# Squares of the first norm added in pairs by VectorE, and uneven halves with TensorE sums in the last norm

## The chip, the cores and the metric

The kernel runs on one core of one Trainium2 chip. A core has five engines that each work through their own list of instructions in order and wait for one another through semaphores: TensorE (PE in the profile, its weight loads PEld), VectorE (DVE), ScalarE (ACT), GpSimd (POOL) and SyncE (SP), which here only issues DMAs. The metric is the device time of one execution in microseconds (us). Before the change the median of three runs was 1303.08 us (1302.94 to 1303.72).

## The reference

One inference step of a one-layer decoder: a prompt of 512 tokens and 8 sequences of 4 new tokens, D_MODEL = 1024. What matters here are its first and its last lines:

```python
def _rms_norm(x, g):
    xf = x.astype(jnp.float32)
    y = xf * lax.rsqrt(jnp.mean(xf * xf, axis=-1, keepdims=True) + RMS_EPS)
    return (y * g).astype(x.dtype)

h = _rms_norm(x, pre_mix_g)          # first norm: everything else needs h
m, new_buf, new_shift, new_wkv = _mixer(h, ...)   # conformer branch, RWKV-7 branch, merge
x = x + _rms_norm(m, post_mix_g)
h2 = _rms_norm(x, pre_ffn_g)
f = jnp.square(jax.nn.relu(h2 @ w_ff_up)) @ w_ff_down
x = x + _rms_norm(f, post_ffn_g)     # last norm: the output y
```

The mean runs over the 1024 channels of a token. All arithmetic is float32.

## The kernel before, in words

Channels lie on partitions, in KT = 8 blocks of 128; tokens lie along the columns. There are N2 = 544 token columns (512 + 32), and N1 = 552 with the 8 rows of shift state. Every product with weights splits both sides into a high and a low part and adds three matmuls (part_steps, L145 to L155; the matmul is L152, its output tile `lin`), so an output block needs 3 matmuls per block of the contracted side. Columns go in two halves: S1 = 276 + 276 in the first norm, S2 = 272 + 272 later.

A sum over channels goes over partitions as well as over blocks. The kernel adds over partitions with a float32 matmul whose weights are a matrix of 1/1024 (`avg`), which leaves the mean in every partition. `rsqrt` (L106 to L112) is then five operations: logarithm and exponential on ScalarE (recorded on L235), a square on ScalarE (L110), and two corrections on VectorE (L111, L112).

The first norm (L254 to L274): eight DMAs bring x, two blocks of half the columns each, with one weight block loaded behind each half. For each half ScalarE squares the eight blocks (L260, tile `sq`, four buffers), and TensorE adds each square into `ss` with a matmul of its own (L261), eight a half. After rsqrt, VectorE scales the blocks to `hf` (L269) and splits them into high and low parts (`xh` by ScalarE, L173; `xl` by VectorE, L174). The first weight products need these, and both halves of them stand in one list on each engine.

The last stage is w_ff_down (L1041 to L1061). Output blocks 0 to 5 are finished with both halves. For each, `down(j)` adds the product to the partial result `part[j]` (tile `f`, VectorE L1028), then acc_sq squares it on ScalarE (L880) and adds the square to `facc` on VectorE (L881). Blocks 6 and 7 (`last`) are held back so that half 0 of both comes first, 96 matmuls of 272 columns, and then half 1 of both. After each half, `rstd` makes one float32 matmul of `avg` with `facc` (L169, tile `aux`) and rsqrt. Then, for each of the eight blocks, VectorE scales it (L1059), adds the residual `m` (L1060), and SP writes it out (L1061). Half 0's closing operations run while TensorE works on half 1's products; half 1's have nothing to run beside.

The order on each engine is set by a scheduler when the program is built; at run time every engine keeps to it. The pool of `lin` tiles in this stage has three PSUM buffers and that of `aux` has two.

Of the kernel before, what the change touches and what calls it, by code (L numbers as in the profile page):

```python
# [8 lines left out]
F32 = mybir.dt.float32  # L9
F32R = mybir.dt.float32r  # L10
AF = mybir.ActivationFunctionType
ALU = mybir.AluOpType
MULT, ADD, SUB = ALU.mult, ALU.add, ALU.subtract

D = 1024
KT = 8
# [21 lines left out]

S1 = ((0, 276), (276, 276))
S2 = ((0, 272), (272, 272))  # L40

VECS = [("pre_mix_g", 8), ("post_mix_g", 8), ("pre_ffn_g", 8), ("post_ffn_g", 8), ("conv_b", 8),
        ("conv_ln_g", 8), ("conv_ln_b", 8), ("decay_base", 8), ("iclr_base", 8), ("k_k", 8),
# [19 lines left out]
def hybrid_step(ctx: ExitStack, tc: tile.TileContext, xT, hist, s0, win, wco, wro, wo, wup, wdn, lora,  # L63
                vecs, convw, cst, yo, convo, shifto, wkvp, wkvs):
    nc = tc.nc
    PSUM = bass.MemoryType.PSUM
    act = nc.scalar.activation
    tt, stt, ts = nc.vector.tensor_tensor, nc.vector.scalar_tensor_tensor, nc.vector.tensor_scalar
# [24 lines left out]
    rms_eps, ln_eps, gn_eps, kk_neg, kk_eps, kk_log = (epst[:, i:i + 1] for i in range(6))  # L93
# [12 lines left out]
    def rsqrt(rs, x, eps, t):  # L106

        tact(LNEXP, rs, x, AF.Ln, bias=eps)
        tact(LNEXP, rs, rs, AF.Exp, scale=-0.5)
        act(t, rs, AF.Square, scale=math.sqrt(0.5))  # L110
        stt(out=t, in0=x, scalar=eps, in1=t, op0=ADD, op1=MULT)  # L111
        stt(out=rs, in0=t, scalar=1.5, in1=rs, op0=SUB, op1=MULT)  # L112

    def con(name):
        o = COFF[name]
        return cs[:, o:o + dict(CONSTS)[name]]
# [3 lines left out]
    def wraw(src):  # L120
        raw = wp.tile([128, KT * 128], F32, name="raw", tag="raw", bufs=WR)
        nc.sync.dma_start(raw, src.rearrange("p k c -> p (k c)"))
        return raw

    def wload(src, paged=None):
        return wsplit(wraw(src), paged)

    def wsplit(raw, paged=None, upper=nc.scalar.copy):

        if paged is None:  # L130
            parts = [(wp.tile([128, KT * 128], F32R, name="whi", tag="whi"),
                      wp.tile([128, KT * 128], F32R, name="wlo", tag="wlo", bufs=WL))]
        else:
            parts = [tuple(paged.tile([128, N2], F32R, name=n, tag="pg") for n in ("wh", "wl")) for _ in range(2)]
        n = KT // len(parts)
        out = []
        for i, (hi, lo) in enumerate(parts):
            r = raw[:, i * n * 128:(i + 1) * n * 128]
            hi, lo = hi[:, 0:n * 128], lo[:, 0:n * 128]
            upper(hi, r)  # L140
            tt(out=lo, in0=r, in1=hi.bitcast(F32), op=SUB)  # L141
            out += [(hi[:, 128 * k:128 * k + 128], lo[:, 128 * k:128 * k + 128]) for k in range(n)]
        return out
# [13 lines left out]
    def part_mm(*args):  # L157
        for _ in part_steps(*args):
            pass
# [72 lines left out]
    def tact(name, *args, **kw):  # L232

        with tables(name):
            lastact[0] = act(*args, **kw)  # L235
        return lastact[0]
# [5 lines left out]
    with tc.tile_pool(name="p0", bufs=1) as p0, tc.tile_pool(name="q0", bufs=1, space=PSUM) as q0:  # L242
        start = tables(LNEXP)
        x = p0.tile([128, KT, N1], F32, name="x")
        for o, m in S1:
            for k in range(0, KT, 2):
                nc.sync.dma_start(x[:, k:k + 2, o:o + m], xT[:, k:k + 2, o:o + m])
            raws.append(wraw(win[order[len(ready)]]))
            ready.append(wsplit(raws[-1]))
        avg = p0.tile([128, 128], F32, name="avg")  # L250
        nc.vector.memset(avg, 1.0 / D)
        rs, rt = (p0.tile([128, N1], F32, name=n) for n in ("rs", "rt"))
        hfs = [p0.tile([128, N1], F32, name=f"hf{k}") for k in range(KT)]
        with start:  # L254
            for s, (o, m) in enumerate(S1):
                q = slice(o, o + m)
                ps = q0.tile([128, 512], F32, name=f"ss{s}")
                for k in range(KT):
                    sq = p0.tile([128, 276], F32, name="sq", bufs=4)
                    act(sq, x[:, k, q], AF.Square)  # L260
                    nc.tensor.matmul(ps[:, 0:m], avg, sq, start=k == 0, stop=k == KT - 1)  # L261
                rsqrt(rs[:, q], ps[:, 0:m], rms_eps, rt[:, q])
            nc.sync.dma_start(cs, cst)
            nc.sync.dma_start(cw, convw)
            for s, (o, m) in enumerate(S1):
                q = slice(o, o + m)
                for k in range(KT):
                    hf = hfs[k]
                    stt(out=hf[:, q], in0=x[:, k, q], scalar=nvec("pre_mix_g", k), in1=rs[:, q], op0=MULT, op1=MULT)  # L269
                    if s:  # L270
                        nc.scalar.copy(hf[:, N2:N1], x[:, k, N2:N1])
                    split_hl(h[k][0][:, q], h[k][1][:, q], hf[:, q])
                    if s:
                        nc.sync.dma_start(shifto[:, k, :], hf[:, T - 1:N2])  # L274
# [51 lines left out]
    def gate(j):  # L326

        i = 50 + j if j < KT else 34 + j
        g = cv.tile([128, N2], F32, name="g", tag="g")
        yield from win_steps(i, S2, lambda s, ps, o, m: nc.scalar.copy(g[:, o:o + m], ps))  # L330
        nc.scalar.dma_start(g_dr[j], g[:, 0:N2])


    with ExitStack() as c1:
# [7 lines left out]
        aux, ytx = dict(pool=qc, tag="aux"), dict(pool=qc, tag="yt")  # L342
# [15 lines left out]
        for i in range(2):  # L358
            q = slice(64 * i, 64 * i + 64)
            nc.scalar.copy(maskD[q, :, i, :], mask[q].rearrange("p (a t) -> p a t", a=2))  # L360
            nc.scalar.copy(maskP[64 * i:64 * i + 32, i, :], maskS[64 * i:64 * i + 32])
            for g in range(2):
                r, o = slice(64 * i + 32 * g, 64 * i + 32 * g + 32), 32 * g
# [53 lines left out]
        def glu_gate(j):  # L417
            sg = page("gsg", cv)
            yield from win_steps(8 + j, S2, lambda s, ps, o, m: nc.scalar.copy(sg[:, o:o + m], ps))
            glu["fresh"], glu["sg"] = (j, sg), sg  # L420

        def glu_val(j, sg):
# [7 lines left out]
            def evac(s, ps, o, m):  # L430
                n = min(m, T - o)
                tt(out=u[:, CW - 1 + o:CW - 1 + o + n], in0=ps[:, 0:n], in1=sg[:, o:o + n], op=MULT)
                if s:
                    tt(out=useg.rearrange("p (b f) -> p b f", f=SEG)[:, :, CW - 1:SEG],
                       in0=ps[:, n:m].rearrange("p (b t) -> p b t", t=TS), in1=sv(sg), op=MULT)
            yield from win_steps(j, S2, evac)
            nc.sync.dma_start(convo[j], u[:, T:EXT])
# [6 lines left out]
        def sum_steps(lhsT, x, evac, pool, tag):  # L444
            for s, (o, m) in enumerate(S2):
                ps = pool.tile([128, 512], F32, name=tag, tag=tag)[:, 0:m]
# [12 lines left out]
        def rates(p):  # L459
# [8 lines left out]
            for i, (d, b) in enumerate(((sg, "decay_base"), (a, "iclr_base"))):  # L468
                for s, (o, m) in enumerate(S2):
                    yield from part_steps([(up[0][:, i], up[1][:, i])], [ld], s, o, m,  # L470
# [293 lines left out]
        def groupnorm(p):  # L764
# [22 lines left out]
            yield  # L787
            for s, (oo, m) in enumerate(S2):
                yield from part_steps([(lhi, llo)], [lg], s, oo, m,
# [69 lines left out]
    ql = c2.enter_context(tc.tile_pool(name="ql", bufs=2, space=PSUM))  # L859
    pl2 = c2.enter_context(tc.tile_pool(name="pl2", bufs=3, space=PSUM))  # L860
# [5 lines left out]
    def temp(name):  # L866
        lc[0] += 1
        pool, tag = ((cv, "t0"), (cv, "t1"), (fp, "t2"))[lc[0] % 3]
        return pool.tile([128, N2], F32, name=name, tag=tag, bufs=1)
    aux = dict(pool=ql, tag="aux")  # L870

    ALL = slice(0, N2)
    HALF = tuple(slice(o, o + m) for o, m in S2)
# [9 lines left out]
    def rstd(rs, acc, eps, s):  # L883
        t = temp("rt")
        f32sum(con("avg"), acc, S2[s:s + 1],
               lambda _, ps, o, m: rsqrt(rs[:, o:o + m], ps, eps, t[:, o:o + m]), **aux)
# [18 lines left out]
    for j in range(KT):  # L905
        o = page("o")
# [14 lines left out]
    with tc.high_priority(offset=HP):  # L921
        acc, mean = keep("acc", "acc"), keep("mean", "rs2")
# [4 lines left out]
        acc = keep("acc", "xacc")  # L927
# [3 lines left out]
        rs = keep("rs", "rs")  # L931
# [36 lines left out]
    acc, xacc, rs, rs2 = (keep(n, n) for n in ("acc", "xacc", "rs", "rs2"))  # L968
# [52 lines left out]
    part = []  # L1021

    def down(j):
        f = part[j]

        def evac(s, ps, o, m):
            q = slice(o, o + m)
            tt(out=f[:, q], in0=ps, in1=f[:, q], op=ADD)  # L1028
            acc_sq(acc, j, f, q)
        return evac  # L1030

    for half in range(2):
        fhl = [None] * 16
# [5 lines left out]
        if half:  # L1039
            acc, rs = keep("facc", "acc"), keep("frs", "rs")  # L1040
        for j in range(KT if half == 0 else KT - 2):  # L1041
            w = wload(wdn[j, 2 * half]) + wload(wdn[j, 2 * half + 1])
            if half == 0:
                f = cv.tile([128, N2], F32, name="f", tag=("gsg", "g")[j]) if j < 2 else \
# [3 lines left out]
            else:  # L1048
                linear(w, fhl, S2, down(j))

    last = [(j, wload(wdn[j, 2], pg) + wload(wdn[j, 3], pg)) for j in (KT - 2, KT - 1)]
    for s in range(2):
        q = HALF[s]
        for j, w in last:
            part_mm(w, fhl, s, *S2[s], down(j), pl2, "lin")
        rstd(rs, acc, rms_eps, s)
        for j in range(KT):
            f = part[j][:, q]
            stt(out=f, in0=f, scalar=nvec("post_ffn_g", j), in1=rs[:, q], op0=MULT, op1=MULT)  # L1059
            tt(out=f, in0=f, in1=x1[j][:, q], op=ADD)  # L1060
            nc.sync.dma_start(yo[:, j, q], f)  # L1061
# [80 lines left out]
```

## Time and profile before

| | us |
|---|---|
| median of 3 runs | 1303.08 (1302.94 to 1303.72) |
| profiled execution, its own time | 1299.37 |
| its span, first to last instruction | 1297.6 |
| TensorE busy | 1238.4 (95%) |
| VectorE busy | 819.9 (63%) |
| ScalarE busy | 652.0 (50%) |
| GpSimd busy | 198.0 (15%) |
| mean granted clock of TensorE | 0.989 |

A timeline row gives start, duration, engine, line, operation, output<-input, shapes and a count; in brackets stands how long the engine sat idle before it and what ended that. Matmuls overlap: a row's duration includes filling and draining, and the distance between starts is what one costs. A float32 matmul with `avg` is recorded as two matmuls (x2). In a table of stretches the columns are the stretch, its length, busy time (number) of each engine, then the granted clock of TensorE (PEclk), the share of DMA and GB/s.

### The profile page before, as it was taken

What the parts mean: (1) busy time and instruction counts of PE and PEld (TensorE: products, weight loads), DVE (VectorE), ACT (ScalarE), POOL (GpSimd) and SP (SyncE); (2) the same over time, 40 slices, a digit from 0 to 9 for tenths busy, and PEclk for the clock granted to TensorE, in tenths of its full rate; (3) what the DMA queues carried; (4) which work ended last, traced back from release to release, by engine and by line L of the source; (5) the groups of instructions that cost most, each with busy time, mean ns of one, the idle gap of its engine ahead of it and who ended that gap; (6) DMA issues with size and microseconds to landing.
All of it is one profiled execution on the core that took longest, in us unless ns stands there. A gap on an engine that the chain in (4) does not pass through costs nothing. (4 is left out here: it accounts for less than half of the span.)

```text
span 1297.6 us, 23134 instructions
## 1 busy us (share of the span) xinstructions
PE 1238.4 (95%) x9154; PEld 1162.8 (90%) x9154; DVE 819.9 (63%) x1545; ACT 652.0 (50%) x1563; POOL 198.0 (15%) x286
## 2 busy tenths in 40 slices
PE   7989999999999999999999999999999999999995
PEld 6978888887978888787889999999999999999995
DVE  6889889855888898887677465658432122333345
ACT  7453747575563747538244382356554223554231
POOL 2224232221323233132201100000000000000000
PEclk9989999999999999999999999999999999999998
DMA  6313121120202121131115642361122332232332
GB/s 202 104 33 109 33 82 34 49 69 19 84 33 96 34 81 33 33 95 42 67 48 195 220 167 92 110 209 50 34 82 82 98 86 94 82 97 75 90 98 70
DMA packets 45181, 110.60 MB, mean 85 GB/s; under 512 B 7056, under 2 KB 16528, under 8 KB 45072
## 3 DMA queue, kind: packets, MB, share of 16 engines
q1 hardware_dynamic: 41344, 104.33, 25.6%
q10 hardware_dynamic: 3728, 4.79, 1.1%
q8 instruction: 72, 1.18, 0.4%
q14 instruction: 37, 0.30, 0.1%
HBM read 94.79 MB, written 14.32 MB: 84 GB/s over the span
## 5 line engine op out<-in xcount | busy, mean ns | idle before, releaser
L152 PE MATMUL lin<-xh,whi 128*128 128x272 f32 (+1 forms) x2096 | 616.2, 294 | 4.1 <-DVE r L394 2.0
L152 PE MATMUL lin<-xh,wlo 128*128 128x272 f32 (+1 forms) x2096 | 615.6, 294 | 0.6 <-DVE wlo L141 0.6
L152 PE MATMUL lin<-xl,whi 128*128 128x272 f32 (+1 forms) x2096 | 614.2, 293 | 0.4 <-DVE xl L174 0.2
L152 PEld LDWEIGHTS lin<-xh,whi 128*128 128x128 f32 x2096 | 397.0, 190 | 7.2 <-issue 2.9
L152 PEld LDWEIGHTS lin<-xl,whi 128*128 128x128 f32 x2096 | 396.5, 189 | 3.7 <-issue 1.4
L152 PEld LDWEIGHTS lin<-xh,wlo 128*128 128x128 f32 x2096 | 396.6, 189 | 3.1 <-issue 1.4
L141 DVE TENSOR_TENSOR wlo<-raw,whi 128x1024 fp32r<-128x1024 f32 x131 | 160.7, 1227 | 197.8 <-ACT whi L140 175.7
L292 DVE SCALAR_TENSOR_TENSOR c<-u,cw,c 128x512 f32<-128x512 f32 x240 | 188.0, 783 | 5.7 <-DVE c L292 1.2
L140 ACT CAST whi<-raw 128x1024 fp32r<-128x1024 f32 x76 | 79.7, 1049 | 122.7 <-PE lin L152 119.2
L140 POOL CAST whi<-raw 128x1024 fp32r<-128x1024 f32 x55 | 65.4, 1189 | 319.0 <-PE lin L152 182.9
L152 PE MATMUL lin<-xh,wl 128*128 128x272 f32 x240 | 69.4, 289 | 0.0
L152 PE MATMUL lin<-xl,wh 128*128 128x272 f32 x240 | 69.3, 289 | 0.0
L152 PE MATMUL lin<-xh,wh 128*128 128x272 f32 x240 | 69.2, 288 | 0.0
L1001 DVE TENSOR_TENSOR xl<-ff,xh 128x272 fp32r<-128x272 f32 x64 | 28.3, 442 | 55.9 <-ACT ff L1000 55.9
L687 ACT ACTIVATE SV<-ch,pc 64x64 f32<-64x64 f32 x128 | 39.6, 309 | 19.2 <-PE ch L683 17.8
L228 ACT ACT_TABLE_LOAD x37 | 47.5, 1283 | 1.8 <-PEq L1124 1.2
L152 PEld LDWEIGHTS lin<-xh,wl 128*128 128x128 f32 x240 | 45.2, 188 | 0.1
L152 PEld LDWEIGHTS lin<-xh,wh 128*128 128x128 f32 x240 | 45.2, 188 | 0.1
L152 PEld LDWEIGHTS lin<-xl,wh 128*128 128x128 f32 x240 | 45.1, 188 | 0.1
L681 ACT ACTIVATE SV<-ch 64x64 f32<-64x64 f32 x128 | 27.9, 218 | 33.6 <-PE ch L679 31.6
L760 POOL TENSOR_SCALAR st<-st,epS 128x64 f32<-128x64 f32 x64 | 39.9, 673 | 7.9 <-DVE rt L597 7.9
L998 ACT ACTIVATE ff<-lin 128x272 f32<-128x272 f32 x64 | 25.3, 395 | 29.6 <-PE lin L152 29.5
(274 smaller groups left out, 1830.4 us busy)
## 6 DMA issues: line engine op xcount, KB each, us to landing
raw<-win SPq DMA_DIRECT2D x58, 512.0 KB, 3.7
raw<-wup SPq DMA_DIRECT2D x32, 512.0 KB, 3.6
raw<-wdn SPq DMA_DIRECT2D x32, 512.0 KB, 3.6
g_dr<-g ACTq DMA_DIRECT2D x16, 272.0 KB, 2.9
raw<-wro SPq DMA_DIRECT2D x8, 512.0 KB, 3.7
raw<-wco SPq DMA_DIRECT2D x8, 512.0 KB, 3.6
raw<-wo SPq DMA_DIRECT2D x8, 512.0 KB, 3.6
x<-xT SPq DMA_DIRECT2D x8, 276.0 KB, 4.7
```

The costliest lines, as they stand in the source:

```text
L140: upper(hi, r)
L141: tt(out=lo, in0=r, in1=hi.bitcast(F32), op=SUB)
L152: nc.tensor.matmul(ps, a, b[:, o:o + m], start=k == 0 and i == 0, stop=k == n - 1 and i == 2)
L228: lastact[0] = nc.scalar.preload_act_table_set(name)
L292: stt(out=c[:, 0:T], in0=u[:, t:t + T], scalar=w[:, t:t + 1], in1=c[:, 0:T], op0=MULT, op1=ADD)
L681: nc.scalar.mul(SV[H[i], c, i, :], ch[H[i], 2, B[i]], -1.0)
L687: nc.scalar.mul(SV[H[i], c + 1, i, :], ch[H[i], 1, B[i]], pc[H[i], c:c + 1])
L760: nc.gpsimd.tensor_scalar(st[:, b, :], st[:, b, :], f["epS"][:, b:b + 1], None, MULT)
L998: act(t[:, q], ps, AF.Relu)
L1001: tt(out=lo[:, q], in0=t[:, q], in1=hi[:, q].bitcast(F32), op=SUB)
```

## The change

Two places change; every instruction between them keeps its place on its engine.

In the first norm the loop takes two blocks at a time, with two tiles `sq0` and `sq1` of three buffers each instead of one of four. In half 0, VectorE squares blocks 1 and 5 itself, and adds the two squares of every pair; TensorE then sums four tiles instead of eight. Half 1 is squared by ScalarE as before and summed in eight matmuls, the second of a pair first.

In the last stage the two blocks held back are cut at column 304 instead of 272 (S3 = 304 + 240). `facc` now holds the squares of blocks 0 to 5 alone: TensorE adds it first, in a matmul with `avg` that opens the sum, and then the squares of blocks 6 and 7 each with a matmul of its own.

```diff
+S3 = ((0, 304), (304, 240))
...
-                for k in range(KT):
-                    sq = p0.tile([128, 276], F32, name="sq", bufs=4)
+                for k in range(0, KT, 2):
+
+                    sq, sq1 = (p0.tile([128, 276], F32, name=f"sq{i}", bufs=3) for i in range(2))
                     act(sq, x[:, k, q], AF.Square)
-                    nc.tensor.matmul(ps[:, 0:m], avg, sq, start=k == 0, stop=k == KT - 1)
+                    if s == 0 and k % 4 == 0:
+                        tt(out=sq1, in0=x[:, k + 1, q], in1=x[:, k + 1, q], op=MULT)
+                    else:
+                        act(sq1, x[:, k + 1, q], AF.Square)
+                    if s == 0:
+                        tt(out=sq, in0=sq, in1=sq1, op=ADD)
+                    else:
+                        nc.tensor.matmul(ps[:, 0:m], avg, sq1, start=k == 0, stop=False)
+                    nc.tensor.matmul(ps[:, 0:m], avg, sq, start=s == 0 and k == 0, stop=k == KT - 2)
                 rsqrt(rs[:, q], ps[:, 0:m], rms_eps, rt[:, q])
...
-    for s in range(2):
-        q = HALF[s]
+    for s, (o, m) in enumerate(S3):
+        q = slice(o, o + m)
+        ps = ql.tile([128, 512], F32, name="aux", tag="aux")[:, 0:m]
+        nc.tensor.matmul(ps, con("avg"), acc[:, q], start=True, stop=False)
         for j, w in last:
-            part_mm(w, fhl, s, *S2[s], down(j), pl2, "lin")
-        rstd(rs, acc, rms_eps, s)
+            part_mm(w, fhl, s, o, m, lambda s, lin, o, m: tt(out=part[j][:, q], in0=lin, in1=part[j][:, q], op=ADD), pl2, "lin")
+            sq = temp("sq")
+            act(sq[:, q], part[j][:, q], AF.Square)
+            nc.tensor.matmul(ps, con("avg"), sq[:, q], start=False, stop=j == KT - 1)
+        rsqrt(rs[:, q], ps, rms_eps, temp("rt")[:, q])
```

In the changed kernel's numbering the new lines are L262 to L271 (first norm) and L1063 to L1077 (last stage): L1066 is the sum of `facc`, L1068 the addition of the product, L1070 the square, L1071 its sum, L1075 and L1076 the two closing operations.

Where rows moved. VectorE at the seam between half 0 and half 1 of the last stage; f_11708 and f_11821 are blocks 6 and 7. Before:

```order
L1060 TENSOR_TENSOR f_11708<-f_11708,m_9174 128x272
L1060 TENSOR_TENSOR f_11821<-f_11821,m_9175 128x272
L1028 TENSOR_TENSOR f_11708<-lin_13894,f_11708 128x272
L881 TENSOR_TENSOR facc_13010<-facc_13010,sq_13944 128x272
L1028 TENSOR_TENSOR f_11821<-lin_13947,f_11821 128x272
L881 TENSOR_TENSOR facc_13010<-facc_13010,sq_13997 128x272
```

And now:

```order
L1076 TENSOR_TENSOR f_11708<-f_11708,m_9174 128x304
L1076 TENSOR_TENSOR f_11821<-f_11821,m_9175 128x304
L1068 TENSOR_TENSOR f_11708<-lin_13896,f_11708 128x240
L1068 TENSOR_TENSOR f_11821<-lin_13949,f_11821 128x240
L112 SCALAR_TENSOR_TENSOR rt_14002<-aux_13894,epst_80,rt_14002 128x240
```

The additions into `facc` are gone; the two additions of half 1's products still stand behind the last closing operations of half 0.

TensorE in half 1, where block 6's products end and block 7's begin (sq_13946 is the square of block 6's half 1; 45 more products of block 7 follow). Now:

```order
L153 MATMUL lin_13896<-xl_12943,wh_13730 128x240
L153 MATMUL lin_13896<-xh_12942,wl_13731 128x240
L153 MATMUL lin_13949<-xh_11922,wh_13738 128x240
L153 MATMUL lin_13949<-xl_11923,wh_13738 128x240
L153 MATMUL lin_13949<-xh_11922,wl_13739 128x240
L1071 MATMUL aux_13894<-sq_13946,cs_74 128x240
L153 MATMUL lin_13949<-xh_11990,wh_13738 128x240
```

Before, no row stood between these products; the only sums were one in half 1 behind its twelfth product and one after the last. Ahead of this place half 1 now also has `facc`'s sum as its first row, and block 7's sum of half 0 behind its second product.

ScalarE at the start, half 0 before:

```order
L260 ACTIVATE sq_158<-x_112 128x276
L260 ACTIVATE sq_161<-x_112 128x276
L260 ACTIVATE sq_164<-x_112 128x276
L260 ACTIVATE sq_167<-x_112 128x276
L140 CAST whi_119<-raw_117 128x1024
L235 ACTIVATE rs_135<-ss0_145,epst_80 128x276
L260 ACTIVATE sq_176<-x_112 128x276
L235 ACTIVATE rs_135<-rs_135 128x276
```

And now:

```order
L266 ACTIVATE sq1_153<-x_112 128x276
L262 ACTIVATE sq0_158<-x_112 128x276
L262 ACTIVATE sq0_164<-x_112 128x276
L266 ACTIVATE sq1_165<-x_112 128x276
L141 CAST whi_119<-raw_117 128x1024
L236 ACTIVATE rs_135<-ss0_145,epst_80 128x276
L262 ACTIVATE sq0_176<-x_112 128x276
L236 ACTIVATE rs_135<-rs_135 128x276
L266 ACTIVATE sq1_177<-x_112 128x276
```

Two squares of half 0 have left ScalarE; half 1's squares still stand behind the logarithm of half 0, with the exponential between the first two.

## The prediction

> **What bounds the kernel now.** I read the page first, for the engines and for the shares of the chain that ended last.
>
> ```profile
> PE 1238.4 (95%) x9154; PEld 1162.8 (90%) x9154; DVE 819.9 (63%) x1545; ACT 652.0 (50%) x1563; POOL 198.0 (15%) x286
> PE 40%; DVE 3%; DMA 2%; ACT 1%; issue 1%; SPq 0%; DVEq 0%; ACTq 0%
> ```
>
> TensorE is at work for 95% of the span, so time is won only where it waits, or after its last matmul. The order of instructions between start and end is the same in both kernels, so two places count. For the end I read the chain that ended last, in order of time (start, us, what).
>
> ```profile
> 1272.52 0.72 PE aux L169 x2
> 1273.25 10.55 PE lin L152 x84
> ...
> 1283.82 0.45 DVE f L1028
> ...
> 1284.76 0.45 DVE facc L881
> ...
> 1285.26 0.74 PE aux L169 x2
> ...
> 1293.98 0.35 DVE f L1060
> ```
>
> TensorE's weight products end at 1283.8; then come the last addition, its square, the sum over blocks, the mean, rsqrt, and sixteen VectorE operations. These 13.8 us to the span's end hide behind nothing. In the half before, one has to see who is late and harms nobody. The timeline of VectorE and ScalarE there:
>
> ```profile
> 1260.80 0.44 DVE L881 TENSOR_TENSOR facc<-facc,sq 128x272 f32<-128x272 f32 x1
> 1271.02 0.44 DVE L1028 TENSOR_TENSOR f<-lin,f 128x272 f32<-128x272 f32 x1 [4.57 <-PE lin L152]
> 1275.75 0.92 DVE L1059 SCALAR_TENSOR_TENSOR f<-f,nvt,frs 128x272 f32<-128x272 f32 x2
> 1281.17 0.78 DVE L1060 TENSOR_TENSOR f<-f,m 128x272 f32<-128x272 f32 x2
> 1281.88 0.43 DVE L1028 TENSOR_TENSOR f<-lin,f 128x272 f32<-128x272 f32 x1
> 1282.34 0.43 ACT L880 ACTIVATE sq<-f 128x272 f32<-128x272 f32 x1 [7.64 <-DVE f L1028]
> ```
>
> And TensorE's:
>
> ```profile
> 1258.80 0.29 PE L152 MATMUL lin<-xh,wh 128*128 128x272 f32 x1
> 1270.82 0.29 PE L152 MATMUL lin<-xh,wh 128*128 128x272 f32 x1
> 1272.21 0.28 PE L152 MATMUL lin<-xh,wl 128*128 128x272 f32 x1
> 1272.88 0.49 PE L152 MATMUL lin<-xh,wh 128*128 128x272 f32 x1
> 1273.21 0.29 PE L152 MATMUL lin<-xl,wh 128*128 128x272 f32 x1
> 1277.48 0.29 PE L152 MATMUL lin<-xh,wl 128*128 128x272 f32 x1
> 1283.50 0.28 PE L152 MATMUL lin<-xh,wl 128*128 128x272 f32 x1
> ```
>
> Half 0 runs from 1258.80 to 1270.82, 96 products in 12.02 us, 0.125 each. In half 1, twelve products go ahead of the sum at 1272.52; the other 36 of block 6 end near 1277.8 (1273.21 is the second, 34 more follow at 0.125). Its addition L1028 could run then, but runs at 1281.88: VectorE is in order and first does half 0's sixteen operations. Those 4.1 us cost nothing, since no matmul waits for that addition.
>
> **The end, part by part.** Let T be the end of half 0's products (1270.82).
>
> Removed: the VectorE additions into facc for the last two blocks. On the path that is one step, 1284.76 to 1285.26, −0.50.
>
> Narrower last half: 32 columns fewer. An element per partition takes VectorE about 1 ns (an estimate, from L1028's 0.44 us for 272 against 0.69 for 512 in the split of the weights).
>
> ```profile
> 1259.20 0.69 DVE L141 TENSOR_TENSOR wl<-raw,wh 128x512 fp32r<-128x512 f32 x1 [1.88 <-ACT wh L140]
> ```
>
> That is 0.033 us an operation, so 16 × 0.033 = 0.53, and 0.26 more on the addition, square, sum and five steps of rsqrt. With the 0.50: **−1.29 behind the last product.**
>
> Added on TensorE: the f32 sums go from two to six. From 1272.52 to 1273.21 less 0.125 one takes 0.56 for 272 columns; scaled, 0.62 for 304 and 0.50 for 240. Products: the half-rate rows below give 0.232 for 272 (3.25/14) against 0.125, so about 0.107 goes with columns, 0.012 for 32 of them: 0.137 and 0.113. The bounds for 240 are 0.110 (in proportion) and 0.125 (no shorter).
>
> Half 0 now: 96 × 0.012 = 1.15, and two sums inside it, 1.24. The first stands behind 13 products (1.78 us) but needs facc's addition, which ended 2.44 after the half began, so 0.7 of waiting; the second, behind eight products of block 7 (1.1), needs block 6's addition and square, 0.1. **+3.2.**
>
> Half 1: TensorE does facc's sum (0.50) and two products, then waits for block 7's square of half 0, as it waited for facc, until T+1.25 (T+1.70 at 1272.52, less 0.50, plus 0.05). With that sum (0.60) and 49 products (5.5) it comes to block 6's sum at T+7.35. That sum needs the square of L1068's addition, which by the order stands behind all sixteen operations of half 0. They ended at T+11.06 (1281.88). Now: −0.50 for the addition that is gone, +0.26 for 32 columns on the steps ahead, +0.53 on the sixteen: T+11.35. Addition and square, 0.43 and 0.44 with their handovers: T+12.22. **TensorE stands still for 4.9 us, with 45 products of block 7 queued behind.** Then 0.50 + 44 × 0.113 puts the last product's start at T+17.69; it was T+12.68. **+5.0.** The narrower columns save nothing ahead of the wait.
>
> The pause has a second price. The granted clock (PEclk) around three pauses, in aligned stretches:
>
> ```profile
> core 0: us, PE busy (x), PEclk, DMA share, GB/s
> 73.26:76.67 3.41, 0.48 (x2) 1.00 0.00 0
> 76.68:83.50 6.82, 5.51 (x21) 0.50 0.00 0
> 336.09:339.50 3.41, 1.48 (x10) 1.00 0.34 130
> 339.50:342.91 3.41, 3.25 (x14) 0.50 0.44 108
> 414.60:418.00 3.40, 2.05 (x19) 1.00 0.44 145
> 418.01:421.42 3.41, 3.41 (x18) 0.50 0.00 0
> ```
>
> A stretch with 1.9 or 1.35 us idle was followed by 3.41 us at half the clock, one with 2.9 us, and 1.3 more of idling, by 6.82, where products take 0.232 and 46% of the time is lost: 1.6 us of 3.41 if all of it falls on work. A 4.9 us pause covers more. Since the drop may begin within the pause, or last two stretches, I bound it between 0.9 and 2.8 (two stretches with 0.8 us of them in the pause); taken, between them, **+2.0**. The Trainium skill, "TensorE: Matmul & The Clock Gate", section "What's actually happening", states that the rate halves after at least one idle window of about 3.4 us, on a free-running grid. By that a 4.9 us pause would hold an entirely idle window in only some 44% of runs (1.5/3.4), and the term would average 0.9. The trace disagrees: the clock fell with 43 and 60% of the stretch busy.
>
> **The start.** ScalarE, VectorE and TensorE in the first 20 us:
>
> ```profile
> 3.99 1.51 ACT L260 ACTIVATE sq<-x 128x276 f32<-128x276 f32 x4 [1.49 <-DMA x<-xT]
> 5.80 0.43 ACT L260 ACTIVATE sq<-x 128x276 f32<-128x276 f32 x1 [0.30 <-PE ss L261]
> 6.72 0.43 ACT L260 ACTIVATE sq<-x 128x276 f32<-128x276 f32 x1 [0.49 <-PE ss L261]
> 10.43 0.49 ACT L235 ACTIVATE rs<-ss,epst 128x276 f32<-128x276 f32 x1 [0.50 <-PE ss L261]
> 3.95 1.06 DVE L100 TENSOR_SCALAR nvt<-vt 128x138 f32<-128x138 f32 x1
> 14.93 0.44 DVE L174 TENSOR_TENSOR xl<-hf,xh 128x276 fp32r<-128x276 f32 x1
> 4.47 5.92 PE L261 MATMUL ss<-sq,avg 128*128 128x276 f32 x16 [4.47 <-ACT sq L260]
> 11.29 4.35 PE L261 MATMUL ss<-sq,avg 128*128 128x276 f32 x16 [0.90 <-ACT sq L260]
> 12.58 2.62 PEld L261 LDWEIGHTS ss<-sq,avg 128*128 128x128 f32 x12 [0.35 <-ACT sq L260]
> 18.79 0.52 PE L152 MATMUL lin<-xh,whi 128*128 128x276 f32 x2 [0.68 <-ACT xh L173]
> ```
>
> The squares at 5.80 and 6.72 wait for TensorE: a sum takes 0.92 us there, and 0.46 later (six in the 2.62 us of weight loads from 12.58). TensorE starts slow; the eight sums from 4.47 to 10.39 (3.7 us at 0.46 each) show about 4 us of it.
>
> Half 0 now has four sums instead of eight. VectorE is free at 5.01; its square and first addition, 0.44 each, put the first sum at 5.97, not 4.47. Four at 0.92 plus 0.36 for filling and draining end at 10.0: **only 0.4 earlier**, since they all run slow. Half 1's sums now take pairs, and the first waits for two squares and the exponential between them (0.64): 11.55 instead of 11.29. Eight at 0.46 end where they ended before. If TensorE is slow again after its 1.5 us rest, half 1 loses 1.7 (3.4 us of it) to 3.7 (all eight), and rsqrt, the casts and the products at 18.79 follow. Before, it rested 0.9 us there and kept its rate; 1.5 is nearer the 1.35 us after which the clock fell. Bounds −0.4 and +3.7; in runs whose grid lies otherwise the old start loses too, so I take **+1.0**. The first cast of weights on ScalarE moves about 0.9 us ahead and with it the third weight DMA on SP; neither is waited for here.
>
> **Sum.** 3.2 + 5.0 + 2.0 − 1.29 + 1.0 = +9.9. The profiled execution took 1299.37 (span 1297.6, 1.8 around it) and would be 1309.3; the runs' median, 1303.08, lies 3.7 above that execution, and the same difference gives **1313.0**.
>
> **Rivals.**
> - *The pause stays at full clock* (a pause that isn't wholly idle for a stretch of the grid doesn't count). For it: the grid's place is chance. Against it: the rows above. 3.2 + 5.0 − 1.29 + 0.5 for the start = +7.4, 1310.5. Chance 0.15. This is the skill's rule just weighed.
> - *Both slow phases run full length*: 3.2 + 5.0 + 2.8 − 1.29 + 3.0 = +12.7, 1315.8. For it: the 6.82 us above; against it: the other two rows. Chance 0.12.
> - *Not slower: VectorE takes block 6's addition ahead of half 0's closing operations.* Then it runs at T+7.2, when its products are done, its square is there at T+8.1, and TensorE waits 0.7; the last product starts at 8.1 + 0.50 + 44 × 0.113 = T+13.6 against T+12.68. 3.2 + 0.9 − 1.29 − 0.4 = +2.4, 1305.5, within what can be told. The same holds if the sixteen operations (6.66 us) were over by T+7.2; they would have to start at T+0.5 rather than T+4.69. Against it: the order, and 1281.88 above, where the old addition already waited 4.1 us. Chance 0.04.
> - *Only the ends shorten* (the sums slip under waits that exist anyway): −0.4 − 1.29 = −1.7, 1301.4. Against it: from 1258.80 to 1283.8 TensorE's only rest is some 0.2 us ahead of the sum at 1272.52. Chance 0.01.
>
> **Numbers.** The forecast has 0.66. Its range alone runs from 1311 (half-clock loss 0.9, start 0.1) to 1315; reaching to the first rival with a start at its low end (1309.6) and to the second (1315.8), it is 1309 to 1316. A difference under 0.2% (2.6 us) can't be told from none. Slower 0.93 (forecast and the first two rivals), same 0.05 (the other two), faster 0.02 (left for what I don't see).
>
> **What would show it.** In the new trace: a TensorE wait of 4 to 5 us for the square of L1070 in the last half, with VectorE busy on L1075 and L1076 throughout; a PEclk of 0.50 in the products behind it; L1068 with 240 columns directly behind the last L1076 with 304. At the start: the logarithm of half 0 near 10.0, the first sum of half 1 near 11.5, and its last between 15.3 and 19. It would be wrong if VectorE interleaved L1068 with half 0's operations, or if the 240-column products reached that sum as late as the addition.

## The result, and the profile after

The changed kernel took **1316.06 us** (median of 4 runs, 1315.54 to 1318.61) beside 1303.01 for the kernel before (1301.37 to 1303.72): a ratio of **1.0109, 95% interval 1.0081 to 1.0137**. It is slower, as forecast, by 13.05 us instead of 9.9. The profiled execution took 1316.54 us, with a span of 1314.8.

The end first. The chain that ended last in the profile after, in order of time (start, us, what):

```profile
1276.49 0.78 PE aux L1071 x2
1277.27 5.60 PE lin L153 x40
1282.90 0.49 DVE f L1068
...
1287.40 0.98 DVE f L1075 x2
...
1293.37 0.77 DVE f L1076 x2
1294.14 0.33 DVE f L1068
1294.49 0.41 ACT sq L1070
1294.95 1.17 PE aux L1071 x2
1296.11 6.16 PE lin L153 x45
1302.29 0.42 DVE f L1068
```

Before, the last stage's products were one row of TensorE from 1273.25 to the end of half 1. Now the chain leaves TensorE at 1282.90, goes through all sixteen closing operations of half 0 on VectorE, and comes back only at 1294.95. TensorE's own timeline names the wait:

```profile
1269.71 0.78 PE L1066 MATMUL aux<-facc,cs 128*128 128x304 f32 x2 [0.40 <-DVE facc L891]
1276.49 0.78 PE L1071 MATMUL aux<-sq,cs 128*128 128x304 f32 x2
1283.97 0.78 PE L1071 MATMUL aux<-sq,cs 128*128 128x304 f32 x2 [0.49 <-ACT sq L1070]
1294.95 1.17 PE L1071 MATMUL aux<-sq,cs 128*128 128x240 f32 x2 [4.68 <-ACT sq L1070]
```

4.68 us without work ahead of block 6's sum. What VectorE did just ahead of the addition L1068 that this sum needs:

```profile
1293.28 0.86 DVE L1076 TENSOR_TENSOR f<-f,m 128x304 f32<-128x304 f32 x2
1294.05 0.41 DVE L1068 TENSOR_TENSOR f<-lin,f 128x240 f32<-128x240 f32 x1
```

The addition starts when the sixteenth operation is done. Behind the pause the granted clock falls, in the table of aligned stretches (stretch, length, TensorE's busy time and instructions, PEclk, DMA share, GB/s):

```profile
1288.03:1291.45 3.42, 2.24 (x20) 1.00 0.29 105
1291.45:1294.86 3.41, 0.00 (x0) 1.00 0.54 192
1294.86:1298.27 3.41, 3.32 (x14) 0.50 0.20 70
1298.27:1301.69 3.42, 3.42 (x32) 1.00 0.00 0
```

The start after, TensorE and then ScalarE:

```profile
5.96 4.05 PE L271 MATMUL ss<-sq,avg 128*128 128x276 f32 x8 [5.96 <-DVE sq L268]
11.55 1.29 PE L270 MATMUL ss<-sq,avg 128*128 128x276 f32 x2 [1.54 <-ACT sq L266]
12.63 1.13 PE L271 MATMUL ss<-sq,avg 128*128 128x276 f32 x2
13.55 1.13 PE L270 MATMUL ss<-sq,avg 128*128 128x276 f32 x2
14.47 0.83 PE L271 MATMUL ss<-sq,avg 128*128 128x276 f32 x2
15.14 0.63 PE L270 MATMUL ss<-sq,avg 128*128 128x276 f32 x2
...
16.53 0.63 PE L271 MATMUL ss<-sq,avg 128*128 128x276 f32 x2
10.05 0.49 ACT L236 ACTIVATE rs<-ss,epst 128x276 f32<-128x276 f32 x1 [0.70 <-PE ss L271]
13.80 0.43 ACT L262 ACTIVATE sq<-x 128x276 f32<-128x276 f32 x1 [0.68 <-PE ss L271]
```

Half 0's four sums take 4.05 us, and half 1's first three still follow one another at 0.92 to 1.08 us; only from the fifth on (15.14) is the distance 0.46. Before, half 1's eight ran at that rate from the first.

**Where the 13 us lie.** I cut every profile at two places that all kernels share, the start of the 150th weight product (`lin`) and the first product of half 0 in the last stage, and added up the stretches of half clock that the records show in between. TensorE works through one and the same list of instructions in the middle part of all these kernels.

| profile (us) | to the 150th product | between | half clock there | last stage |
|---|---|---|---|---|
| before | 37.9 | 1220.9 | 20.5 | 38.8 |
| after | 41.2 | 1226.2 | 23.9 | 47.4 |

So against this profile of before: +3.3 at the start, +8.6 in the last stage, and +5.3 in a part that the change doesn't touch. The experiments show what to make of each.

### The profile page after: what moved, and what is told of

Same layout as the page of the kernel before. It is cut to its first block, busy times and chain, and to the rows that moved or that the text cites. A ratio compares the mean times of both kernels' runs of the same rounds, so it can differ in the third digit from the quotient of the medians.

```text
span 1314.8 us, 23134 instructions
## 1 busy us (share of the span) xinstructions
PE 1245.5 (95%) x9154; PEld 1168.3 (89%) x9154; DVE 821.8 (63%) x1547; ACT 651.6 (50%) x1561; POOL 197.8 (15%) x286
## 5 line engine op out<-in xcount | busy, mean ns | idle before, releaser
L153 PE MATMUL lin<-xh,wl 128*128 128x272 f32 (+2 forms) x240 | 70.4, 293 | 0.0
L153 PE MATMUL lin<-xl,wh 128*128 128x272 f32 (+2 forms) x240 | 70.1, 292 | 0.0
L153 PE MATMUL lin<-xh,wh 128*128 128x272 f32 (+2 forms) x240 | 70.0, 292 | 0.0
```

Of the source, the lines that this page charges most:

```text
L153: nc.tensor.matmul(ps, a, b[:, o:o + m], start=k == 0 and i == 0, stop=k == n - 1 and i == 2)
```

## The experiments

The first four take the change apart. In the diffs, `add` stands for `lambda s, lin, o, m: tt(out=part[j][:, q], in0=lin, in1=part[j][:, q], op=ADD)`.

**1. The start alone:** the first norm's loop as changed, the last stage as before.

```diff
-                for k in range(KT):
...
+                for k in range(0, KT, 2):
...
```

> The change of the first norm alone; the last stage as before. Theory A (half 1's sums run at the slow rate again, and the rest of the start follows; +3.2 us by the time the products flow, as the changed kernel's trace shows at 31 us): +2 to +4 us against before, first sum of half 1 near 11.5, its last near 17. Theory B (the first norm costs the predicted +1.0 and the other losses of the changed kernel's trace, 5.7 us between start and end, are chance of that execution): +0.5 to +1.5. Theory C (those 5.7 us follow from the first norm, because everything behind it meets other waits): +6 or more, with the same jumps near 718 and 760 us.

Median 1304.65 beside 1303.57, ratio 1.0000 (0.9977 to 1.0023): about +1 by the medians, and not to be told from none. Theory C's +6 is shut out; Theory B and the low end of Theory A both lie within the interval. Its profile shows how bad the start can get, though:

```profile
5.93 2.21 PE L270 MATMUL ss<-sq,avg 128*128 128x276 f32 x4 [5.93 <-DVE sq L267]
12.34 1.29 PE L269 MATMUL ss<-sq,avg 128*128 128x276 f32 x2 [1.55 <-ACT sq L265]
...
18.02 0.82 PE L269 MATMUL ss<-sq,avg 128*128 128x276 f32 x2
18.93 0.49 PE L152 MATMUL lin<-xh,whi 128*128 128x276 f32 x1
```

The first six of half 1's sums run slow, and the first weight product starts at 18.93.

**2. The last stage alone:** the first norm as before.

```diff
-    for s in range(2):
+    for s, (o, m) in enumerate(S3):
...
+            nc.tensor.matmul(ps, con("avg"), sq[:, q], start=False, stop=j == KT - 1)
```

> The change of the last stage alone; the first norm as before. Theory A (in the changed kernel's trace the last stage grew from 38.8 to 47.1 us): +8.3 us, a TensorE wait of about 4.7 us for the square of block 6 in half 1, PEclk 0.50 behind it. Theory B (the last stage costs its own 8.3 and also what comes before it): more than +10. If the half clock is the chance that the prediction gave it, a run without it would be near +6.5.

1313.15 beside 1303.57, ratio 1.0078 (1.0051 to 1.0105): +9.6. Most of the loss is here; the interval, +6.6 to +13.7, holds both theories. In its profile the pause is 4.70 us, with half clock behind it.

**3. The pause taken away:** experiment 2 with block 6's sum of half 1 placed behind block 7's products. The same sums, the same widths, the same VectorE order; only TensorE has nothing to wait for in the middle of the half.

```diff
             act(sq[:, q], part[j][:, q], AF.Square)
-            nc.tensor.matmul(ps, con("avg"), sq[:, q], start=False, stop=j == KT - 1)
+            if s == 0 or j == KT - 1:
+                for z in held + [sq]:
+                    nc.tensor.matmul(ps, con("avg"), z[:, q], start=False, stop=j == KT - 1 and z is sq)
+            else:
+                held.append(sq)
```

> As the last stage changed alone, but half 1's sum of block 6's square stands behind block 7's products instead of ahead of 45 of them; VectorE's order stays as it is, and the same sums are made. If the wait for VectorE is the cause, the 4.7 us pause and the half clock behind it are gone: half 0 +3.2, half 1 about -0.3 to its last product, end -1.3: +1.6 against before, +1 to +2.5. If the added sums and the uneven cut were the cost, it stays near +8.

1304.69 beside 1303.57, ratio 1.0001 (0.9981 to 1.0021): no loss is left that can be told. Half 1's two sums in its TensorE timeline:

```profile
1288.41 0.57 PE L1064 MATMUL aux<-sq,cs 128*128 128x240 f32 x2
1289.51 0.67 PE L1064 MATMUL aux<-sq,cs 128*128 128x240 f32 x2 [0.53 <-ACT sq L1061]
```

Block 6's square has long been there at 1288.41, and half 1 takes 12.10 us from its first product to its last, against 19.06 in the profile after. The last stage as a whole is 40.6 us, against 48.2 in experiment 2 and 38.8 before. So the wait for VectorE's place in line is the cause of most of the loss. Of the rest, the wider half 0 with its extra sums costs 3.75 us, and half 1 and the end win 1.9 of it back.

**4. The uneven halves alone:** 304 + 240 columns, the squares added into `facc` as before.

```diff
-            part_mm(w, fhl, s, *S2[s], down(j), pl2, "lin")
-        rstd(rs, acc, rms_eps, s)
+            part_mm(w, fhl, s, o, m, add, pl2, "lin")
+            acc_sq(acc, j, part[j], q)
+        t = temp("rt")
+        f32sum(con("avg"), acc, S3[s:s + 1], lambda _, ps, o, m: rsqrt(rs[:, q], ps, rms_eps, t[:, q]), **aux)
```

> The uneven cut 304 + 240 alone: squares are added to facc by VectorE and summed once a half, as before. By the prediction's prices the last half's closing is 0.8 us shorter, half 0's products 1.15 longer and half 1's 1.15 shorter. VectorE would finish half 0's sixteen operations near T+11.85, so block 6's addition, square and sum end near T+13.2, later than block 7's products (T+12.0): 0.5 to 1.2 us of the gain goes there. Expected -0.3 to +0.7. If 240 columns were no cheaper than 272, +1.0 to +2.

1304.87 beside 1303.57, ratio 1.0005 (0.9984 to 1.0027). Its last stage is 39.3 us in the profile, +0.6 on before: half 0 loses 1.4, the steps behind the last product win 0.8. The split by itself neither wins nor loses anything that can be told.

**5. The whole change again,** since +9.6 and +1.1 make 10.7 and the whole had measured 13.05.

> The changed kernel itself, once more, with five rounds. Theory A (the sum of the parts): the last stage alone measured +9.6 us and the start alone +1.1, so the whole is about +10.7, a median of 1313 to 1315 beside 1303 to 1304, and the 1316.06 of its four first runs lay high by the luck of those runs. Theory B (the parts hinder each other, or the change costs more than its parts): the median stays at 1316 or above, +12.5 to +13.5.

1315.2 (six runs) beside 1301.5, ratio 1.0101 (1.0077 to 1.0125). The difference, +13.7, is Theory B's; the median lies just above Theory A's range and under Theory B's. So the first result was not the luck of four runs. The interval, +10.0 to +16.3, does not shut out +10.7. Whether the parts hinder each other, or one of them was measured too low alone, is what 9 to 11 are for.

**6. The pause filled:** experiment 2 with 40 products of 240 columns in the place where TensorE stood still. They read weights and inputs that lie there anyway, and their result is used nowhere.

```diff
+            if s and j == KT - 2:
+                idle = pl.tile([128, 512], F32, name="idle", tag="lin")
+                for _ in range(40):
+                    nc.tensor.matmul(idle[:, 0:240], w[0][0], fhl[0][0][:, 304:544], start=True, stop=True)
             nc.tensor.matmul(ps, con("avg"), sq[:, q], start=False, stop=j == KT - 1)
```

> The change of the last stage alone (+9.6 us), with 40 products of 240 columns put on TensorE ahead of block 6's sum, in the 4.7 us in which it stood still; their result is used nowhere. They take 40 x 0.113 = 4.5 us at full clock. Theory A (the pause has a second price, the half clock behind it, 0.9 to 2.8 us): no stretch of half clock behind that place, and 1.5 to 2.5 us less than the last stage alone, so +7 to +8. Theory B (the half clock costs next to nothing or would have come anyway): +9 to +10. Theory C (VectorE's and ScalarE's work lengthens beside a busy TensorE, or the products are done later than the square): more than +10.

1310.3 beside 1301.5, ratio 1.0064 (1.0040 to 1.0087): +8.8, which by the times alone could be either theory. The profile decides it. TensorE's timeline:

```profile
1284.70 4.65 PE L1064 MATMUL idle<-xh,wh 128*128 128x240 f32 x40
1289.90 0.67 PE L1065 MATMUL aux<-sq,cs 128*128 128x240 f32 x2 [0.55 <-ACT sq L1060]
```

And its clock in aligned stretches, all at full speed where the change had half:

```profile
1284.73:1288.15 3.42, 3.42 (x33) 1.00 0.55 194
1288.15:1291.56 3.41, 2.86 (x24) 1.00 0.45 162
1291.56:1294.97 3.41, 3.41 (x33) 1.00 0.00 0
```

Block 6's sum comes 12.03 us after the first product of the half, as in the profile after, so the filling delayed nothing and Theory C falls. Half 1 takes 17.81 us here from first to last product. In the four profiles with the pause left empty it took 19.06, 19.10, 19.80 and 19.98. So the half clock behind the pause costs 1.25 to 2.2 us, 1.7 on average, and the wait itself 17.81 − 12.68 = 5.1.

**7. The start filled:** experiment 1 with idle products of 128 columns by the averaging matrix, 11 ahead of the first sum and 6 between the halves.

```diff
+            idle = q0.tile([128, 512], F32, name="idle")
+            for _ in range(11):
+                nc.tensor.matmul(idle[:, 0:128], avg, avg, start=True, stop=True)
...
+                for _ in range(0 if s else 6):
+                    nc.tensor.matmul(idle[:, 0:128], avg, avg, start=True, stop=True)
                 rsqrt(rs[:, q], ps[:, 0:m], rms_eps, rt[:, q])
```

> The change of the start alone (+1.1 us), with 11 products of 128 columns by the averaging matrix ahead of the first sum and 6 between the halves; their result is used nowhere. Theory A (TensorE is slow in its first 4 us of work, and its rest between the halves makes it slow again): the four sums of half 0 take 0.46 us each instead of 0.92, the logarithm of half 0 comes near 8.3 instead of 10.05, half 1's sums all take 0.46, and the first weight product moves 1 to 2.5 us ahead of the unfilled start's, for a total of -1.5 to 0 against the kernel before. Theory B (the squares and additions set the pace, not the rate of TensorE): the logarithm stays within 0.5 us of 10.0 and the total at +1.

1299.89 beside 1301.5, ratio 0.9990 (0.9971 to 1.0009). TensorE and ScalarE in the start:

```profile
1.22 5.06 PE L257 MATMUL idle<-avg 128*128 128x128 f32 x22 [1.22 <-DVE avg L251]
6.08 1.25 PE L273 MATMUL ss<-sq,avg 128*128 128x276 f32 x4
...
11.57 0.73 PE L272 MATMUL ss<-sq,avg 128*128 128x276 f32 x2 [1.02 <-ACT sq L268]
12.14 0.63 PE L273 MATMUL ss<-sq,avg 128*128 128x276 f32 x2
...
15.23 0.49 PE L152 MATMUL lin<-xh,whi 128*128 128x276 f32 x1
7.86 0.43 ACT L264 ACTIVATE sq<-x 128x276 f32<-128x276 f32 x1 [1.56 <-DMA x<-xT]
9.12 1.04 ACT L140 CAST whi<-raw 128x1024 fp32r<-128x1024 f32 x1 [0.50 <-DMA raw<-win]
10.07 0.48 ACT L235 ACTIVATE rs<-ss,epst 128x276 f32<-128x276 f32 x1
```

All sums are quick now, and half 1 gets its rate back: the first weight product starts at 15.23 instead of 16.79 to 18.93. Theory A held for half 1 and failed for half 0. The logarithm of half 0 stays where it was in this execution, at 10.07, because with quick sums the last squares wait for x itself (7.86) and the logarithm for a cast of weights that ScalarE has taken on in between (from 9.12). Here other work ends last, and fewer sums in half 0 could not have won anything. It is not so in every execution: in experiment 11, with the same start, the cast comes at 8.37 and the logarithm at 9.32.

**8. What was of use so far, put together:** the kernel before with 8 idle products ahead of its first squares, and in half 1 only block 7's square summed by TensorE, `facc` (with block 6's square) while VectorE adds block 7's product.

```diff
+            for _ in range(8):
+                nc.tensor.matmul(idle[:, 0:128], avg, avg, start=True, stop=True)
...
+            part_mm(w, fhl, s, *S2[s], add, pl2, "lin")
+            nc.tensor.matmul(ps, con("avg"), acc[:, q], start=True, stop=False)
...
+            nc.tensor.matmul(ps, con("avg"), sq[:, q], start=False, stop=True)
```

> The kernel before with what the experiments so far leave of use: even halves and half 0 as before; in half 1 block 6's addition and square go into facc as before, facc is summed by TensorE while VectorE adds block 7's product, and only block 7's square has a TensorE sum of its own; and eight idle products of 128 columns ahead of the first squares at the start. Theory A: behind the last product the step of adding into facc (0.50 us) is gone, and the start gains 1 to 1.7 us because the first sums no longer run slow: -1.5 to -2.2 us. Theory B (the first sums wait for the squares, not for TensorE's rate): -0.5 us alone, which can't be told from no change.

1301.56 beside 1301.5, ratio 0.9991 (0.9971 to 1.0010): inconclusive. In its profile the last stage is 38.3 us, 0.5 shorter, as both theories had it, and the start 37.5.

The last four ask whether the named causes account for the whole, in the whole change.

**9. The whole change with the late sum** of experiment 3.

> The whole change, but in half 1 block 6's square is summed behind block 7's products, so that TensorE has nothing to wait for there. Cut at the 150th weight product and at the first product of the last stage, the profiles so far give: start 41.3 us on average in three profiles with the changed start, 38.95 in five with the old one; last stage 38.8 us before, 47.4 to 47.6 with the change, 40.6 in the late-sum run; the stretch between is the same in all and varies from 1220.9 to 1227.5 whatever the kernel. Theory A (the change costs the sum of its parts: +2.4 at the start, +8.7 in the last stage, of which the wait and the half clock behind it are 6.9): +2.4 + 1.8 = +4.2. Theory B (the two parts together cost 2 to 3 us more than alone, which is why the whole measured +13): +6 or more.

1308.06 beside 1305.41, ratio 1.0022 (1.0001 to 1.0043), +2.7: under Theory B's +6, which the interval (up to +5.6) shuts out; Theory A's +4.2 lies inside it.

**10. The whole change with the start filled** as in experiment 7.

> The whole change, with the 17 idle products of 128 columns at the start (11 ahead of the first sum, 6 between the halves; their result is used nowhere). Theory A (the start's cost is TensorE's low rate in half 1's first sums, gone when it does not rest): start 37.8 us to the 150th product instead of 41.3, which is 1.15 under the old start's average, and +8.7 in the last stage: +7.5. Theory B (parts hinder each other): +10 or more.

1310.79 beside 1305.41, ratio 1.0047 (1.0028 to 1.0065), +5.4: not the +10 of Theory B; Theory A's +7.5 lies inside the interval (+3.7 to +8.5). The pause is there as before (4.68 us), and what followed it, in aligned stretches:

```profile
1278.08:1281.50 3.42, 0.64 (x6) 1.00 0.53 189
1281.50:1284.90 3.40, 1.50 (x5) 0.50 0.50 179
1284.90:1288.30 3.40, 3.40 (x18) 0.50 0.00 0
```

The same 4.7 us, lying otherwise on the grid, give two stretches of half clock in place of one.

**11. Both at once.**

> The whole change with both named causes taken away: the late sum in half 1, and the 17 idle products at the start. Theory A: -1.15 + 1.85 = +0.7, no difference that can be told from the kernel before, so that the two causes account for all of the loss. Theory B (something else in the change costs 2 to 3 us): +3 or more.

1302.52 beside 1305.41, ratio 0.9986 (0.9966 to 1.0005). No loss is left that can be told, and Theory B falls here a third time. Two terms cancel here: in its profile the last stage is still 1.6 us longer than before (40.4 against 38.8), and the filled start 1.9 shorter than the old start's average (37.1 against 38.95). So the two named causes account for the loss but for those 1.6 us.

**12. The kernel before with 8 idle products ahead of its squares.**

```diff
+            idle = q0.tile([128, 512], F32, name="idle")
+            for _ in range(8):
+                nc.tensor.matmul(idle[:, 0:128], avg, avg, start=True, stop=True)
```

> The kernel before with 8 idle products of 128 columns ahead of its first squares and nothing else. Theory A (the old start, too, loses 0 to 2.8 us to TensorE's low rate, as the clock happens to lie): 37.5 us to the 150th product as in the run with the last sum, 1.4 under the old start's average of 38.95, and -1 to -1.5 in all. Theory B (the old start loses nothing that counts): within 0.5 us of the kernel before.

1301.61 beside 1305.41, ratio **0.9974 (0.9956 to 0.9992)**: quicker than the kernel before, by an interval that just excludes 1. The profile supports about −1.5 of the 3.8 (37.4 us to the 150th product against 38.95 on average), and runs 7 and 8 with filled starts gave 0.9990 and 0.9991 with intervals that reach 1, so its true size is nearer the small end.

**All cuts together.** The columns are those of the first table; the rows are grouped by start.

| start | to the 150th product | mean |
|---|---|---|
| old (before, 2, 3, 4, 6) | 37.9, 40.7, 38.2, 40.2, 37.8 | 38.95 |
| changed (after, 1, 5, 9) | 41.2, 41.8, 40.9, 41.9 | 41.5 |
| filled (7, 8, 10, 11, 12) | 37.8, 37.5, 37.6, 37.1, 37.4 | 37.5 |

| last stage | us | mean |
|---|---|---|
| old (before, 1, 7, 12) | 38.8, 38.8, 38.8, 38.8 | 38.8 |
| changed (after, 2, 5, 10) | 47.4, 48.2, 47.6, 48.0 | 47.8 |
| pause filled (6) | 46.3 | |
| late sum (3, 9, 11) | 40.6, 40.5, 40.4 | 40.5 |

The part between took 1218.3 us (10) to 1227.9 (9), 1223.75 on average over 14 profiles, with 17.1 and 30.7 us of half clock in it for the shortest and the longest. The whole part as one stretch (TensorE's busy time and instructions, PEclk, DMA share, GB/s), in experiment 10:

```profile
37.61:1255.95 1218.34, 1181.01 (x8780) 0.99 0.26 83
```

and in experiment 9:

```profile
41.91:1269.85 1227.94, 1186.61 (x8779) 0.99 0.26 82
```

The same products, with 5.6 us more of TensorE's busy time and 4.0 more without work.

With that mean in the middle and 1.8 us around the span, the means of the two tables give each kernel a time, which stands beside its measured median:

| kernel | start + 1223.75 + last stage + 1.8 | measured |
|---|---|---|
| before | 1303.3 | 1303.01, 1303.57, 1301.5, 1305.41 |
| whole change | 1314.8 | 1316.06, 1315.2 |
| 1, start alone | 1305.8 | 1304.65 |
| 2, last stage alone | 1312.3 | 1313.15 |
| 3, late sum | 1305.0 | 1304.69 |
| 9, change with late sum | 1307.5 | 1308.06 |
| 10, change with start filled | 1310.8 | 1310.79 |
| 11, both | 1303.5 | 1302.52 |
| 12, before with start filled | 1301.8 | 1301.61 |

All medians lie within 2.2 us of the sum of three parts; the largest gap is the kernel before's own, in the series of experiments 9 to 12. Part by part is how this kernel's changes are to be weighed; the difference of two medians is coarser.

## Why the prediction was right in its mechanism, and which step failed

**The wait in half 1: right.** It named the place (block 6's sum), the holder (VectorE's sixteen closing operations, in order), and 4.9 us; the trace has 4.68, 4.70, 4.67 and 4.68 in four profiles. It put +5.0 on half 1, and with the pause filled half 1 is 5.1 longer. That it is the cause is shown by experiment 3, which removes the wait, and with it the half clock behind it, and nothing else. The rival in which VectorE takes the addition first falls with the rows at 1293.28 and 1294.05; the one in which only the ends shorten falls with the time.

**The half clock behind the pause: right, a little large.** +2.0 was taken between 0.9 and 2.8; the four profiles show 1.25, 1.3, 2.0 and 2.2. The clock fell behind four of four pauses, so the rival with full clock falls. By the Trainium skill, "TensorE: Matmul & The Clock Gate", section "What's actually happening", it takes an idle window. The profile after has such a stretch, with 0.00 us of work (1291.45 to 1294.86). Experiment 10 has 0.64 us of work in the stretch ahead and got two halved ones: here a wholly idle stretch was not needed.

**Half 0 and the end: right.** Half 0 took 15.57 us against 12.02, +3.55 for the +3.2 forecast: forty products of 304 columns take 5.60, so 0.140 each rather than 0.137, 0.3 over 96. Behind the last product 12.77 against 14.08, −1.31 for −1.29. The last stage as a whole averages 47.8, **+9.0 against a forecast of 3.2 + 5.0 + 2.0 − 1.29 = 8.9**.

**The start: the step that failed.** The prediction said: "in runs whose grid lies otherwise the old start loses too, so I take +1.0." The averages say 41.5 − 38.95 = **+2.5**. The bounds (−0.4 to +3.7) held it, and the times it gave are met (logarithm near 10.0, then 10.05; first sum of half 1 near 11.55, then 11.55; last between 15.3 and 19, then 16.53). The fault was in asking whether TensorE would be slow *again* after its rest. It had never become quick. Old starts do half 0's eight sums in one run of 5.8 to 6.9 us (five profiles), and in each of them half 1 ran at 0.46 from its first sum. The changed start has four sums in 4.05 us and then 1.54 of rest, and in none of four profiles was TensorE quick when half 1 began. The clock records of the traces begin with the rise to full clock, where the distance between sums goes from 0.92 to 0.46: at 8.19 to 10.76 us in the five old starts, at 14.86 to 18.39 in the four changed ones. Nor is it only the chance of the grid: in three changed starts (after, 1, 5) and one old one (6) the grid lies at the same place to 0.15 us, and they rose at 14.86, 18.39, 14.92 and 8.19.

The first product then starts at 17.5 on average instead of 15.75. The same section of the Trainium skill says that full speed comes after a busy window of about 3.4 us on a free-running grid. By that, an estimate from the measured lengths, four slow sums in 4.05 us cover a whole window in (4.05 − 3.41)/3.41 = 19% of executions. Eight slow sums would take 4.05 + 4 × 0.92 = 7.7 us, more than two windows, and so cover one wherever the grid lies. The traces agree: five of five against none of four. This is the rule that spoke against the change, and the prediction used only its other half. The other 0.8 us of the 2.5 come at 20 to 25 us, where three of the four changed starts and two of the five old ones have another halved stretch; nine profiles can't tell whether that is the change or chance.

**The sum.** With 2.5 for 1.0 and 9.0 for 8.9, the change costs 11.5. The prediction had 1313.0, and its upper end of 1316 was passed by 0.06; the second measurement, 1315.2, lies under it. Of the 3.15 us between 13.05 and 9.9 the start accounts for 1.5 and the last stage for 0.1; about 1.5 lies in no part.

The range was too narrow for a plain reason: it was made of the bounds of single costs, and left out that the part between changes by 9.6 us from execution to execution. The prediction did meet this, as the 3.7 us by which the profiled execution lay under the median, and rightly added it: that profile had one of the shortest middle parts (1220.9, mean 1223.75) and one of the shorter starts.

**The rival with both slow phases in full** had the nearest number, 1315.8, for a mechanism of which half is seen: the start's sums ran slow nearly throughout in one of four profiles (1), but the half clock behind the pause never cost its 2.8.

**Not settled.** 1314.8 by the parts leaves about 1 us of the measured medians open, less than the part between varies by. And the start alone, 1.0000, holds +2.5 only near the end of its interval (1.0023 is 3 us); the averages of four and five profiles are as coarse. Another cure, VectorE's addition of block 6 put ahead of the closing operations, was not tried.

## What to carry to other kernels

Ahead of a wait that looks harmless ask what sits behind it: the old addition waited 4.1 us for VectorE's closing operations and cost nothing, until a matmul was made to need its result and 45 products queued up. Move the consumer behind independent work (here one sum by 45 products, −7 us); speeding the producer was not tried. And count TensorE's work at the start by its unbroken length: halving the sums left runs too short to bring it to speed, and slowed the next eight by more than they saved.

## What the runs showed of the hardware

I had not expected one unchanged list of 6,667 weight products and their company to take anything from 1218.3 to 1227.9 us. Longer times go largely with more half clock, whose stretches come in lengths of 3.41, 6.8 and 10.2 us on a 3.41 us grid that lies elsewhere in each execution: 17.1 us of them in the shortest, 20.5 in six from 1220.9 to 1222.8, 27 to 34 in four from 1225.1 to 1227.9. It is not all of the difference: the longest has 13.6 us more of half clock than the shortest, which costs at most half of that, 6.8 of 9.6 us, and three with 23.9 lie between 1223.7 and 1226.2. That the place of this kernel's short waits on the grid decides is my reading, and not shown. A change worth less than 3 us can't be seen in a handful of executions.

And idle work can pay. Eight products that compute nothing, placed where TensorE had nothing to do, gave the kernel before 1301.61 us beside 1305.41, of which its profile supports about 1.5, and forty others took the half clock from behind a 4.7 us pause.
